# A 3-D average pooling kernel: the first load moved ahead of the sync engine's register instructions

## The chip, the cores and the metric

The kernel runs on one core of one Trainium2 chip. The time is the device time of one execution in microseconds (us), as the median of several executions. I compare only executions that alternated in one session on one chip.

## The reference

```python
def setup_inputs():
    batch, channels, d, h, w = (8, 32, 32, 32, 32)
    kernel_size = 2
    ...
# each output is the mean of a 2x2x2 window:
result[:, :, i, j, k] = np.mean(window, axis=(-3, -2, -1))
```

In: 33.55 MB of float32. Out: 4.19 MB.

## The kernel before

The 256 (batch, channel) rows fill 128 partitions twice. Each half is read in pieces of up to 128x8192 elements (4 MB), all issued by SyncE (SP) on one queue into five buffers. VectorE does three passes on each piece: add pairs along depth (line 58), pairs along width (line 62), pairs along height with the factor 0.125 (line 65). Three stores follow.

```python
    for t, k0, parts in plan:
        tin = pool_in.tile([P, 32 * KF], F32, tag="tin", name="tin")
        ...
            nc.sync.dma_start(                      # line 77: the ten loads
                out=v, in_=xv[t * P:(t + 1) * P, (k0 + o) * KF:(k0 + o + kb) * KF])
        ...
            pool_unit(v, t, k, kb)                  # VectorE, three passes
    for t, k0, kb in [(0, 0, 16), (1, 0, 14), (1, 14, 2)]:
        nc.sync.dma_start(...)                      # line 86: the three stores
```

While the source edits it, the program opens with a common block: six register instructions on each engine (a zero, the core's base address, four bounds), then a barrier of all engines. The kernel already lifts its first load, which waits for nothing, out of the program into that opening block, just ahead of SP's part of the barrier (SP's drain):

```python
    opening, program = blocks[0].instructions, blocks[tc.starting_block_idx].instructions
    load = next(i for i in program if isinstance(i, mybir.InstDMACopy))
    assert load.engine == nc.sync.engine
    barrier = next(
        n for n, i in enumerate(opening)
        if i.engine == load.engine and isinstance(i, mybir.InstDrain))
    program.remove(load)
    opening.insert(barrier, load)
```

Of the kernel before, what the change touches and what calls it, by code (L numbers as in the profile page):

```python
# [1 line left out]

# [4 lines left out]

F32 = mybir.dt.float32
KF = 256


@with_exitstack
def pool_rows(
    ctx: ExitStack,
    tc: tile.TileContext,
    x: bass.AP,
    kernel_size: int,
    out: bass.AP,
):
    nc = tc.nc  # L20
    assert kernel_size == 2, "only kernel_size == 2 supported"

    B, C, D, H, W = x.shape
    P = nc.NUM_PARTITIONS
    assert (B * C, D, H, W) == (2 * P, 32, 32, 32)
    add = mybir.AluOpType.add



    xv = x.rearrange("b c d h w -> (b c) (d h w)")  # L30
    ov = out.rearrange("b c d h w -> (b c) (d h w)")




    pool_in = ctx.enter_context(tc.tile_pool(name="pin", bufs=5))
    pool_out = ctx.enter_context(tc.tile_pool(name="pout", bufs=1))
    obuf = [pool_out.tile([P, 16 * KF], F32, name=f"obuf{t}") for t in range(2)]
    dummy = pool_out.tile([P, 1], F32, name="dummy")


    plan = [
        (0, 0, (32,)),
        (0, 32, (32,)),
        (0, 64, (32,)),
        (0, 96, (32,)),
        (1, 0, (32,)),
        (1, 32, (32,)),
        (1, 64, (16, 16)),
        (1, 96, (16, 16)),  # L50
    ]

    def pool_unit(buf, t, k0, kb):

        od = kb // 8
        a = buf.rearrange("p (o dd e) -> p o dd e", o=od, dd=2)
        b = buf[:, :od * 1024]
        nc.vector.tensor_add(  # L58
            out=b.rearrange("p (o e) -> p o e", o=od), in0=a[:, :, 0], in1=a[:, :, 1])
        bv = b.rearrange("p (e ww) -> p e ww", ww=2)  # L60
        c = buf[:, od * 1024:od * 1536]
        nc.vector.tensor_add(out=c, in0=bv[:, :, 0], in1=bv[:, :, 1])  # L62
        cv = c.rearrange("p (j hh k) -> p j hh k", hh=2, k=16)
        o0 = k0 * KF // 8
        nc.vector.tensor_tensor_reduce(  # L65
            out=obuf[t][:, o0:o0 + od * 256].rearrange("p (j k) -> p j k", k=16),
            in0=cv[:, :, 0], in1=cv[:, :, 1],
            scale=0.125, scalar=0.0, op0=add, op1=add, accum_out=dummy[:, :],
        )

    for t, k0, parts in plan:
        tin = pool_in.tile([P, 32 * KF], F32, tag="tin", name="tin")
        views = []
        o = 0
        for kb in parts:
            v = tin[:, o * KF:(o + kb) * KF]
            nc.sync.dma_start(
                out=v, in_=xv[t * P:(t + 1) * P, (k0 + o) * KF:(k0 + o + kb) * KF])
            views.append((v, k0 + o, kb))
            o += kb  # L80
        for v, k, kb in views:
            pool_unit(v, t, k, kb)


    for t, k0, kb in [(0, 0, 16), (1, 0, 14), (1, 14, 2)]:
        nc.sync.dma_start(
            out=ov[t * P:(t + 1) * P, k0 * KF:(k0 + kb) * KF],
            in_=obuf[t][:, k0 * KF:(k0 + kb) * KF],
        )


def kernel(tc: tile.TileContext, x: bass.AP, kernel_size: int, out: bass.AP):
    nc = tc.nc
    pool_rows(tc, x, kernel_size, out)
    tc.close()
    tc.compile()  # L96
    blocks = nc.main_func.blocks



    opening, program = blocks[0].instructions, blocks[tc.starting_block_idx].instructions
    load = next(i for i in program if isinstance(i, mybir.InstDMACopy))
    assert load.engine == nc.sync.engine
    barrier = next(
        n for n, i in enumerate(opening)
        if i.engine == load.engine and isinstance(i, mybir.InstDrain))
    program.remove(load)
    opening.insert(barrier, load)


# [1 line left out]
_INS = ['x', 'kernel_size']  # L112
_OUTS = [((8, 32, 16, 16, 16), 'float32')]

_NUMBERS = {'kernel_size': 2}


# [26 lines left out]
```

## Time and profile before

| | before |
|---|---|
| median of 3 executions | 93.52 us (93.45 to 93.53) |
| profiled execution | 93.1 us, span 91.3 us |
| transfers | 37.75 MB, 413 GB/s over the span |
| VectorE busy | 64.0 us, 70% of the span |
| first load | issued at 0.00, landed at 12.05 us |

The span runs from the first recorded instruction to the last; the device time is some 1.8 us longer (93.1 against 91.3). How to read it: the transfers are busy from end to end, VectorE waits for loads, and the chain that ended last begins with the load that the change moves. The prediction shows the lines.

### The profile page before, as it was taken

What the parts mean: (1) busy time and instruction counts of PE and PEld (TensorE: products, weight loads), DVE (VectorE), ACT (ScalarE), POOL (GpSimd) and SP (SyncE); (2) the same over time, 40 slices, a digit from 0 to 9 for tenths busy, and PEclk for the clock granted to TensorE, in tenths of its full rate; (3) what the DMA queues carried; (4) which work ended last, traced back from release to release, by engine and by line L of the source; (5) the groups of instructions that cost most, each with busy time, mean ns of one, the idle gap of its engine ahead of it and who ended that gap; (6) DMA issues with size and microseconds to landing.
All of it is one profiled execution on the core that took longest, in us unless ns stands there. A gap on an engine that the chain in (4) does not pass through costs nothing.

```text
span 91.3 us, 103 instructions
## 1 busy us (share of the span) xinstructions
DVE 64.0 (70%) x40; POOL 0.2 (0%) x4
## 2 busy tenths in 40 slices
DVE  0000079974999299939995699749999999999300
POOL 0000000000000000000000000000000000000000
DMA  8998799999997899999997999989999999999992
GB/s 230 459 445 373 344 445 459 459 459 459 459 445 344 373 445 459 459 459 459 459 431 330 388 459 459 459 345 459 445 395 423 459 431 395 409 409 436 427 395 84
DMA packets 1872, 37.75 MB, mean 413 GB/s; under 512 B 208, under 2 KB 208, under 8 KB 336
## 3 DMA queue, kind: packets, MB, share of 16 engines
q1 hardware_dynamic: 1872, 37.75, 97.2%
HBM read 33.55 MB, written 4.19 MB: 413 GB/s over the span
## 4 chain that ended last, share of the span: by engine, by line
DMA 58%; DVE 35%; issue 0%; DVEq 0%
DMA tin<-in_x_dram 58%; DVE tin L58 19%; DVE tin L62 10%; DVE obuf L65 6%; DVE dummy L65 0%; DVEq L96 0%
## 5 line engine op out<-in xcount | busy, mean ns | idle before, releaser
L58 DVE TENSOR_TENSOR tin<-tin 128x4096 f32<-128x4096 f32 (+1 forms) x10 | 35.7, 3569 | 20.5 <-DMA tin<-in_x_dram 20.5
L62 DVE TENSOR_TENSOR tin<-tin 128x2048 f32<-128x2048 f32 (+1 forms) x10 | 18.6, 1864 | 0.3
L65 DVE CUSTOM_DVE_ANT_1 obuf<-tin 128x1024 f32<-128x1024 f32 (+1 forms) x10 | 10.1, 1011 | 0.3
L65 DVE DVE_READ_ACCUMULATOR2_ANT dummy<- 128x1 f32 x10 | 0.8, 82 | 0.0
L125 POOL MEMSET const-bfloat16-1.0<- 128x1 bf16 x1 | 0.1, 101 | 0.0
L125 POOL MEMSET const-uint8-127<- 128x1 uint8 x1 | 0.1, 101 | 0.0
L125 POOL MEMSET const-float32-0.0<- 128x1 f32 x1 | 0.1, 98 | 0.2 <-issue 0.2
L125 POOL MEMSET const-float32-1.0<- 128x1 f32 x1 | 0.1, 98 | 0.0
## 6 DMA issues: line engine op xcount, KB each, us to landing
tin<-in_x_dram SPq DMA_DIRECT2D x6, 4096.0 KB, 34.9
tin<-in_x_dram SPq DMA_DIRECT2D x4, 2048.0 KB, 38.0
out_dram<-obuf SPq DMA_DIRECT2D x1, 2048.0 KB, 36.2
out_dram<-obuf SPq DMA_DIRECT2D x1, 1792.0 KB, 8.8
out_dram<-obuf SPq DMA_DIRECT2D x1, 256.0 KB, 5.1
```

Source lines behind the costliest of these rows:

```text
L58: nc.vector.tensor_add(out=b.rearrange("p (o e) -> p o e", o=od), in0=a[:, :, 0], in1=a[:, :, 1])
L62: nc.vector.tensor_add(out=c, in0=bv[:, :, 0], in1=bv[:, :, 1])
L65: nc.vector.tensor_tensor_reduce(out=obuf[t][:, o0:o0 + od * 256].rearrange("p (j k) -> p j k", k=16), in0=cv[:, :, 0], in1=cv[:, :, 1], s ...
L125: nc = _bacc.Bacc("TRN2", target_bir_lowering=False, num_devices=1)
```

## The change

The intent is to start the first transfer sooner by taking it past the six register instructions that stand ahead of it on SP.

```diff
     load = next(i for i in program if isinstance(i, mybir.InstDMACopy))
-    assert load.engine == nc.sync.engine
-    barrier = next(
-        n for n, i in enumerate(opening)
-        if i.engine == load.engine and isinstance(i, mybir.InstDrain))
+    assert load.engine == nc.sync.engine and load.regs_accessed() == ((), ())
+    assert not load.sync_info.on_wait
+    first = next(n for n, i in enumerate(opening) if i.engine == load.engine)
     program.remove(load)
-    opening.insert(barrier, load)
+    opening.insert(first, load)
```

## The prediction

> **What bounds the kernel now.** I read the page first (span, slices, chain), then the chain in order of time, then a table of stretches, and last what stands around the opening. The first view is the page of the kernel before:
>
> ```profile
> span 91.3 us, 103 instructions
> DVE 64.0 (70%) x40; POOL 0.2 (0%) x4
> ...
> DMA  8998799999997899999997999989999999999992
> ...
> HBM read 33.55 MB, written 4.19 MB: 413 GB/s over the span
> ...
> DMA 58%; DVE 35%; issue 0%; DVEq 0%
> ```
>
> To see here: the DMA engines are 7 to 9 tenths busy in 39 of 40 slices, VectorE only 70% of the span. The kernel is a stream of 37.75 MB through one DMA queue. The chain of waits in order of time says which work carries the end:
>
> ```profile
> 0.00 12.05 DMA tin<-in_x_dram
> ...
> 20.12 40.49 DMA tin<-in_x_dram
> 60.61 0.02 issue
> 60.63 4.44 DVE tin L58
> ```
>
> The columns are start, duration, what. The chain starts at 0.00 with the very load that the change touches, and 12.05 us pass until it has landed and VectorE may begin. The piece at 20.12 is the sixth load, released by the first tile's last VectorE instruction; its landing at 60.61 starts the last uninterrupted VectorE stretch. The table of stretches (start:end, length, DVE busy, POOL busy, clock, DMA share, GB/s) completes it:
>
> ```profile
> 0.00:2.00 2.00, 0.00 (x0) 0.20 (x4) 1.00 0.93 262
> 2.00:12.00 10.00, 0.00 (x0) 0.00 (x0) 1.00 0.97 419
> 12.00:22.00 10.00, 8.18 (x5) 0.00 (x0) 1.00 0.97 419
> 22.00:60.60 38.60, 31.57 (x16) 0.00 (x0) 1.00 1.00 431
> 60.60:85.20 24.60, 24.29 (x20) 0.00 (x0) 1.00 1.01 426
> 85.20:91.30 6.10, 0.00 (x0) 0.00 (x0) 1.00 0.67 283
> ```
>
> From 2.0 to 85.2 us the transfers run at 419 to 431 GB/s with no hole. In 60.6 to 85.2 VectorE is busy too (24.29 of 24.60 us), but that stretch begins with a landing. So the whole schedule hangs on the moment of the first issue: if the first load starts d earlier against the launch, I expect the end nearly d earlier. The slope is 1; the question is how large d is.
>
> **What the skill says.** (1) "Perfetto Trace Analysis", section "Per-instruction lifecycle: what the profiler-reported window actually captures", says that a hardware-generated DMA's window on the issuing queue covers only locking the descriptor generator, generating, and the sequencer's semaphore push, with the data movement outside. The trace agrees: the ten loads' issue windows are 327 to 501 ns (rows of line 77), while landing takes 12.1 us for the first. Moving an issue therefore moves the 12 us behind it, not just some 0.4 us. (2) The same page, section "Roofline", gives 16 DMA engines about 435 GB/s together. The stretches at 419 to 431 sit just below; single slices of the page show 459, so the measurement is the one to take, and it says that the stream is full. (3) "Runtime: NRT & Kernel Launch", section "Instruction fetch mechanics", puts a register loaded from HBM at about 200 ns. That bears on one of the six instructions, which loads the core's base address into two registers; the other five are register moves. No row of this trace is such a load, so the trace neither confirms nor denies it.
>
> **The change part by part.** It removes no work and adds none. In the kernel's own list of the opening, the first load stands behind SP's six register instructions and ahead of SP's drain; the change puts it ahead of the six.
>
> Step 1, is anything left to be jumped over? I compared the programs that the two kernels are built to, engine by engine. On SP both read: the load, a drain, a semaphore wait, a branch, then the other 12 transfers. The six register instructions are in neither: nothing in this program reads those registers, and they are gone when the program is written out. The compiled instruction streams of all five engines are the same byte for byte; only line numbers for debugging differ (the new source is one line shorter). The load was moved ahead of instructions that do not survive.
>
> Step 2, does the trace agree? The rows of line 125 (the opening barrier) and the head of the timeline:
>
> ```profile
> 0.00 2.66 SPq L77 DMA_DIRECT2D tin<-in_x_dram  x5
> 0.23 0.10 POOL L125 MEMSET const-float32-0.0<- 128x1 f32 x1 [0.23 <-issue]
> ```
>
> ```profile
> L125 DVEq DRAIN  x1: 10/10/10, 0.1 to 0.1; - x1
> L125 ACTq DRAIN  x1: 8/8/8, 0.1 to 0.1; - x1
> L125 SPq DRAIN  x1: 142/142/142, 0.4 to 0.4; - x1
> ```
>
> The load is the first record of the whole execution, ahead of the other engines' first drains at 0.1. And the page's 103 instructions can be added up: 40 on VectorE, 4 memsets, 12 other rows at line 125, 13 at line 77 (10 loads, 3 waits), 5 at line 86 (3 stores, 2 waits), 29 at line 96 (the closing barriers). 40 + 4 + 12 + 13 + 5 + 29 = 103, with no register instruction among them. A count alone would not prove it, since a profile may leave such instructions out; with the streams being equal it is enough.
>
> Step 3, the sum: instructions removed in front of the load 0, so d = 0 us. Off the path: nothing changes either. 93.52 us - 0 = 93.5 us.
>
> **The rivals.** Rival A: the six do run before and the load really gains their time. Size, an estimate: SP's closing waits and drains (line 96) follow one another about 65 ns apart in the trace (the first wait at 90.3 us, the sixth row at 90.6), so five moves are 0.3 us; the base load adds two registers at the 200 ns of the "Runtime" page, 0.4 us. d would be about 0.7 us and the time 92.8 us, still within 2% (which begins below 91.65 us). Against it: the built streams. Rival B: issued as the very first instruction, the load meets a queue or a descriptor generator that is not ready, and costs up to some tenths: 93.6 to 94.0. Against it: it is SP's first instruction already in the trace of before. Rival C: d is real but hidden, because the barrier of the opening or VectorE's tail sets the end. The barrier is over by 0.7 us, and the five first issues by 2.66, far ahead of the landing at 12.05, so it would stay hidden; it makes 93.5 as well and differs from my theory only if there is a d. Rival D: the same program simply times differently on another chip or at another hour. This is the only one that I think can show: the three runs spread 93.45 to 93.53, and the run under the profiler took 93.1, 0.4 us lower.
>
> **Range and chances.** The centre is the median of before. The width is only repetition: 0.08 us within one set, 0.4 us to the profiled run. I take 93.2 to 93.8. For faster or slower by over 2% something would have to move by 1.87 us, more than twice Rival A's whole estimate and more than four times the seen spread. I leave 1% on either side for a disturbed set of runs.
>
> **What would show it.** Right: in the profile after, 103 instructions again, the load at 0.00 and the first drains of the other engines at 0.1, VectorE's first instruction near 12.1 us, a span within 0.3 us of 91.3, and the opening rows of the same durations. Rival A would show as a first drain of the other engines clearly later against the load (0.7 instead of 0.1 us) and a time near 92.8. Rival B would show a first landing later than 12.3 us after the issue. I would be wrong if times differ by over 0.3 us in the same session in alternating runs while the streams are equal: then the premise that equal streams take equal time fails, for instance through where the program or its arrays lie in memory.

## The result, and the profile after

| | before | after |
|---|---|---|
| median, first session, 6 executions each | 93.43 us (93.2 to 93.53) | 93.49 us (93.35 to 93.71) |
| span of the profiled execution | 91.3 us | 91.9 us |

The ratio is 1.0012 with a 95% interval of 0.9993 to 1.0032, so the time is the same. A ratio here is the mean time of one kernel's fast runs over that of the other's of the same rounds, so it is not quite the ratio of the medians quoted.

From the page after, with the same fields as the lines of before:

```profile
span 91.9 us, 103 instructions
DVE 64.1 (70%) x40; POOL 0.2 (0%) x4
...
DMA  8999889999999988999999987999999999999992
...
HBM read 33.55 MB, written 4.19 MB: 411 GB/s over the span
```

Again 103 instructions. The head of the timeline (start, duration, queue, line, operation):

```profile
0.00 2.61 SPq L77 DMA_DIRECT2D tin<-in_x_dram  x5
0.23 0.10 POOL L124 MEMSET const-float32-0.0<- 128x1 f32 x1 [0.23 <-issue]
```

And the opening's rows, which are now line 124 because the source is one line shorter (count, durations in ns as min/median/max, first and last start):

```profile
L124 DVEq DRAIN  x1: 10/10/10, 0.1 to 0.1; - x1
L124 ACTq DRAIN  x1: 8/8/8, 0.1 to 0.1; - x1
L124 SPq DRAIN  x1: 133/133/133, 0.4 to 0.4; - x1
```

The load stands at 0.00 in both executions, and the other engines' drains follow at 0.1 in both. In the single records behind these rows, the starts of the next nine after the load differ by 1 or 2 ns between the two kernels; the tenth, SP's drain, starts at 432 ns in both and lasts 133 instead of 142 ns. Nothing was jumped over.

The two profiled executions differ by 0.6 us nevertheless, and one should know where. Two tables of stretches (start:end, length, DVE busy, POOL busy, clock, DMA share, GB/s), before:

```profile
12.00:60.00 48.00, 39.75 (x20) 0.00 (x0) 1.00 0.99 429
60.00:75.00 15.00, 14.26 (x10) 0.00 (x0) 1.00 1.00 427
75.00:80.00 5.00, 4.93 (x5) 0.00 (x0) 1.00 1.01 410
80.00:85.00 5.00, 4.90 (x6) 0.00 (x0) 1.00 0.99 426
```

After:

```profile
12.00:60.00 48.00, 39.74 (x20) 0.00 (x0) 1.00 0.99 428
60.00:75.00 15.00, 14.31 (x10) 0.00 (x0) 1.00 1.02 429
75.00:80.00 5.00, 4.93 (x5) 0.00 (x0) 1.00 1.01 370
80.00:85.00 5.00, 4.71 (x6) 0.00 (x0) 1.00 0.98 419
```

Up to 75 us the two are alike; the first landing is even 0.05 us earlier after (12.00 against 12.05). The difference arises between 75 and 80 us, while the last load is under way: 370 against 410 GB/s. The last load landed at 81.11 us after and at 80.48 before. It is not a property of the change: over the nine profiled executions the first nine landings, counted from the first issue, agree within 0.4 us, while the tenth lies anywhere between 80.5 and 81.1.

The DMA share of that stretch is 1.01 in both tables: the engines were not short of work, their packets took longer. A packet of the last loads takes 0.61 us (median). In all nine profiles, 15 to 31 of them took 0.70 to 1.28 us instead, and nearly all of these started between 76.7 and 79.4 us: 15 in before, which has the earliest tenth landing, and 26 in after, which has the latest. The last landing of the whole program then follows the tenth load by 9.81 to 9.83 us in all nine. So the lateness goes straight through to the end by the transfers, while VectorE ends only 0.22 us later (85.42 against 85.20).

This small lateness alters the look of the chain of waits. After:

```profile
0.73 0.07 issue
0.79 0.33 SPq L77
1.13 0.05 issue
1.18 30.24 DMA tin<-in_x_dram
...
39.86 41.25 DMA tin<-in_x_dram
81.11 0.02 issue
81.13 2.30 DVE tin L58
```

In before's chain, VectorE's last stretch began at 60.63. Here VectorE idled 0.2 us for the last load, so the chain is followed back through that load instead, and its share for transfers goes from 58% to 78%. A reader who compared only these shares would see a new bottleneck. Both chains belong to one schedule: the last load lands 0.44 us before VectorE asks for it in the one, and 0.2 us after in the other. Neither chain shows the end itself, which is the stores' landing at 90.31 and 90.93 us.

### The profile page after: what moved, and what is told of

The parts are those of the page before. It is cut to its first block, busy times and chain, and to the rows that moved or that the text cites. A ratio compares the mean times of both kernels' runs of the same rounds, so it can differ in the third digit from the quotient of the medians.

```text
span 91.9 us, 103 instructions
## 1 busy us (share of the span) xinstructions
DVE 64.1 (70%) x40; POOL 0.2 (0%) x4
## 4 chain that ended last, share of the span: by engine, by line
DMA 78%; DVE 13%; SPq 1%; issue 0%; DVEq 0%
DMA tin<-in_x_dram 78%; DVE tin L58 7%; DVE tin L62 4%; DVE obuf L65 2%; SPq L77 1%; DVE dummy L65 0%; DVEq L96 0%
```

## The experiments

The theory: the compiled streams are equal, so the change does nothing (the instruction files of all five engines are the same byte for byte); the first issue sets the end one for one, and what comes behind it has slack. Rivals: a small real effect hidden in the spread; register instructions that cost nothing anyway; early delays that are made up later; a barrier or a queue depth that matters.

**1. The changed kernel again, five alternating rounds.** No edit.

> The changed kernel once more, unaltered, five alternating rounds. My theory (the compiled streams are the same byte for byte, so the change does nothing): ratio to the kernel before within 0.3% of 1 on either side, profile with 103 instructions, other engines' first drains 0.1 us after the load. Rival (the change has a small real effect, of either sign, hidden by the first session's spread of 93.2 to 93.7): the same sign as in the first session, ratio about 1.0012, with an interval that leaves out 1.

Measured: 93.43 us (6 executions) against 93.46 us (11 executions of before). Ratio 0.9993, interval 0.9977 to 1.0009. The sign turned round against the first session and both intervals hold 1. There is no small effect that these runs can see.

**2. The six register instructions kept, ahead of the load.** This asks whether the idea would have been right if there had been something to jump over. The edit to the kernel before gives the registers a reader at the program's end. That reader is itself an empty instruction and is gone from the built program, but the six writers stay:

```diff
+    sp = nc.sync
+    base = sp.tpb_base_reg
+    regs = [sp.zero_reg, base.lo, base.hi] + [r for p in sp.bc_regs for r in (p.lo, p.hi)]
+    sp.keepalive_nop([sp.lower_val_access(r) for r in regs])
```

> The kernel before, with an empty instruction at the program's end that reads the seven registers, so that SP's six register instructions stay in the program and stand ahead of the load, as the intent of the change takes them to. If the six are costly and all that was missing is that they had been removed: slower than the kernel before by about 0.7 us (my estimate: five moves of 65 ns and one base load of 0.4 us), so about 94.2 us. Rival (register instructions cost SP next to nothing, or the measured time begins only with the first transfer): within 0.2 us of the kernel before. If the profile records register instructions, its count rises from 103 to 109.

Measured: 93.71 us against 93.46 us, ratio 1.0026, interval 1.0006 to 1.0046 (0.06 to 0.43 us). The page and the opening's rows show the six:

```profile
span 91.9 us, 109 instructions
```

```profile
L130 SPq MOVE  x5: 29/29/36, 0.0 to 0.3; - x5
...
L130 SPq BASE_LOAD  x1: 12/12/12, 0.1 to 0.1; - x1
...
L130 SPq DRAIN  x1: 128/128/128, 0.8 to 0.8; - x1
```

```profile
0.37 2.60 SPq L77 DMA_DIRECT2D tin<-in_x_dram  x5
12.42 4.43 DVE L58 TENSOR_TENSOR tin<-tin 128x4096 f32<-128x4096 f32 x1 [12.42 <-DMA tin<-in_x_dram]
```

So the profile does record register instructions: 103 + 6 = 109. The count of 103 in before therefore shows by itself that none ran there. The load's issue moved from 0.00 to 0.37 us, and VectorE's first instruction from 12.08 to 12.42. Neither of my two numbers fits well. The cost is real (0.25 us between the medians, 0.37 us at the issue, which the interval holds), but it is half or less of my 0.7 us.

**3. The six kept, the load first.** The same edit on the changed kernel.

> The changed kernel with the same six kept: the load first, then the six, then the drain. This is the change with something to jump over. My theory: the time of the kernel before within 0.2 us, since the six now run while the first load's bytes are on the way, and only delay the opening barrier and loads 2 to 5 (needed at 12 us and later). Rival (the opening barrier matters as well): slower than the kernel before by the six's cost, as much as the sibling with the six ahead.

Measured: 93.36 us against 93.46 us, ratio 0.9987, interval 0.9971 to 1.0003. The opening's rows and the timeline:

```profile
L129 SPq MOVE  x5: 29/29/40, 0.4 to 0.8; - x5
...
L129 SPq BASE_LOAD  x1: 49/49/49, 0.5 to 0.5; - x1
```

```profile
0.00 2.99 SPq L77 DMA_DIRECT2D tin<-in_x_dram  x5
...
12.01 4.42 DVE L58 TENSOR_TENSOR tin<-tin 128x4096 f32<-128x4096 f32 x1 [12.01 <-DMA tin<-in_x_dram]
```

The six now run from 0.4 to 0.8 us, behind the load, and cost nothing that can be measured. Runs 2 and 3 differ only in the place of the load, as the two kernels were meant to: 93.71 - 93.36 = 0.35 us, close to the 0.37 us of the shifted issue, and their intervals against before do not overlap. So in this kernel with its register instructions kept alive, the change would have worked and been worth about 0.4%; each of the two medians rests on six executions that spread over 0.4 to 0.7 us.

**4. The load not lifted at all.** The statements that lift the load are removed from the kernel before; nothing else changes.

```diff
-    opening, program = blocks[0].instructions, blocks[tc.starting_block_idx].instructions
-    load = next(i for i in program if isinstance(i, mybir.InstDMACopy))
...
-    program.remove(load)
-    opening.insert(barrier, load)
```

> The load is not hoisted at all: it stays the first instruction of the program, behind the opening barrier. It measures the slope: what a known delay of the first issue costs at the end. The issue comes some 0.6 to 0.8 us later than in the kernel before. Theory (one full stream of transfers, slope 1): the time rises by about that much, to 94.1 to 94.3 us. Rival (the delay is absorbed by VectorE's tail or a faster start of the queue): under 0.2 us.

Measured: 94.13 us against 93.46 us, ratio 1.0072, interval 1.0056 to 1.0087 (0.52 to 0.81 us). The timeline:

```profile
0.73 2.35 SPq L77 DMA_DIRECT2D tin<-in_x_dram  x5
12.87 4.42 DVE L58 TENSOR_TENSOR tin<-tin 128x4096 f32<-128x4096 f32 x1 [12.87 <-DMA tin<-in_x_dram]
```

Issue 0.73 us later, end 0.67 us later. The slope of about 1 holds for a delay of known size.

**5. A long register chain ahead of the load, and 6. the same chain behind it.** Both edit the changed kernel; the two differ in one line. A first attempt with additions only was folded to a single instruction by the build; alternating additions and multiplications are packed six to an instruction.

```diff
+    count = sp.alloc_register("count")
+    sp.reg_mov(count, 0)
+    for n in range(ADDS):                       # ADDS = 96
+        (sp.reg_mul if n % 2 else sp.reg_add)(count, count, 3)
+    sp.keepalive_nop([sp.lower_val_access(count)])
...
+    at = opening.index(load)                    # behind: opening.index(load) + 1
+    opening[at:at] = chain
```

> The changed kernel with a dependent chain of 96 additions and multiplications of one register (kept alive by a reader at the program's end; the build packs six into one instruction, so one move and 16 instructions) ahead of the load. It doubles or more the delay of the six register instructions (0.37 us in the run with the six ahead). Let X be the time from the first record to the load's issue, read from this run's profile; at 50 to 200 ns for each packed instruction X is 0.9 to 3.3 us. Theory (slope 1): the time is 93.4 us plus X within 0.3 us. Rival (part of an early delay is made up later): clearly less than X.

> The same chain directly behind the load, ahead of SP's drain. Theory (only the first issue is on the path): 93.4 us within 0.3 us, although the opening barrier and loads 2 to 5 come X later, as long as load 2 is issued before load 1's last packets at some 11 us. Rival (the barrier or the depth of the queue matters): slower by up to X.

Measured, against 93.25 us for the kernel before in the same rounds: ahead 95.38 us, ratio 1.0214, interval 1.0189 to 1.024 (1.76 to 2.24 us; clear of 1); behind 93.46 us, ratio 1.0013, interval 0.9993 to 1.0033. The timelines, ahead first:

```profile
1.96 2.66 SPq L78 DMA_DIRECT2D tin<-in_x_dram  x5
14.14 4.43 DVE L59 TENSOR_TENSOR tin<-tin 128x4096 f32<-128x4096 f32 x1 [14.14 <-DMA tin<-in_x_dram]
```

```profile
0.00 4.45 SPq L78 DMA_DIRECT2D tin<-in_x_dram  x5
...
12.11 4.42 DVE L59 TENSOR_TENSOR tin<-tin 128x4096 f32<-128x4096 f32 x1 [12.11 <-DMA tin<-in_x_dram]
```

X is 1.96 us. The interval against before holds it (the medians differ by 2.13 us), and ahead minus behind is 95.38 - 93.46 = 1.92 us: the slope once more. The 50 to 200 ns for a packed instruction in the expectation was a guess; they start 115 ns apart. Behind the load, the same chain makes the issues of loads 1 to 5 last until 4.45 instead of 2.66 us and delays the barrier with them, and no change of the time is seen. What lies behind the first issue is off the path.

**7. All five free loads ahead of the barrier.** An attempt to gain on both kernels.

```diff
+    loads = [i for i in program if isinstance(i, mybir.InstDMACopy)][:5]
...
+    opening[first:first] = loads
```

> The changed kernel with all five loads that wait for nothing ahead of the opening barrier. Theory: 93.4 us within 0.2 us, since the loads behind the first one have some 10 us to spare and the first one is where it was. Rival (a deeper queue in the first microseconds fills the slow start of the transfers, whose first packets take 1.9 instead of 1.2 us): 92.8 to 93.2 us.

Measured: 93.37 us against 93.25 us, ratio 1.0008, interval 0.9987 to 1.003. The five issues end at 2.37 instead of 2.66 us, and it brings nothing. The rival falls: the first 16 packets still take 1.43 to 2.19 us (1.30 to 2.10 in before), so the queue's slow start is not for want of loads behind the first. No run pointed to a version that beats both kernels, so there is none here.

Four starts of the first load in one table. The end is the landing of the last store, counted from the first issue, in the profiled execution. The medians come from three sessions (before had 93.46 and 93.25 us in the other two), so compare them only roughly:

| kernel | first issue, us | last landing after it, us | median, us |
|---|---|---|---|
| before (first profile) | 0.00 | 90.3 | 93.52 |
| six kept, ahead | 0.37 | 90.5 | 93.71 |
| not lifted | 0.73 | 90.7 | 94.13 |
| chain ahead | 1.96 | 90.8 | 95.38 |

The other five profiles have the issue at 0.00 and end 90.6 to 90.9 us after it. The spread of 90.3 to 90.9 is the spread of repetition described above; the rest of the schedule simply moves with the first issue.

## Why the prediction was right

- **Step 1 (nothing left to jump over) was right.** Giving the six a reader brought them back (run 2). The equal streams gave equal times within 0.12% in two sessions, with opposite signs.
- **Step 2 (the trace agrees) was right, and stronger than I claimed.** I held that a count of 103 would not prove it, since the profile might leave register instructions out. Run 2 shows that it records them.
- **Step 3 (d = 0, 93.5 us) was right:** 93.49 us, in the range.
- **The slope of 1 was right:** 0.73 us gave 0.67 us, and 1.96 us gave 1.92 us against the sibling kernel.
- **One of its signs did not come true:** a span within 0.3 us of 91.3. It was 91.9, with equal streams. I had taken the span of the one before profile as the mark, but that profile has the earliest end of all nine (90.3 us after the first issue; the others 90.5 to 90.9). So this sign could not tell the change from repetition.
- **The single slices of 459 GB/s were misread.** The page books a whole packet to the slice in which it starts, and 32 packets of 32 KB in a slice of 2.28 us make 459. Landings tell the rate better: loads 2 to 6 land 9.7 us apart, which is 432 GB/s, below the 435 that the prediction cites.
- **Rival A was mis-sized.** Two terms of it: five moves at 65 ns, and 0.4 us for the base load. In run 2 the records start at 0, 93, 140, 194, 253, 304 ns and the load at 374 ns; so the six cost 0.37 us, about 62 ns each. From the base load's start to the next start it is 47 ns in run 2 and 85 ns in run 3, where moves take 51 to 97 ns. The 200 ns that I took from the "Runtime" page is for a register loaded from memory, and two of those do not fit this instruction.
- **Rival B** (a queue that is not ready) shows no sign. The first load landed 11.99 to 12.12 us after its issue in the runs where it was SP's first instruction, and 12.02 (run 2), 12.12 (run 4) and 12.16 us (run 5) where others had run before it.
- **Rival C** (a real d, hidden by the barrier or VectorE's tail) fell, and the prediction argued it badly: that the barrier is over long before the landing means that it can't hide anything. Runs 3 and 6 delay the barrier and change nothing that can be seen; runs 2, 4 and 5 delay the first issue, and it shows.
- **Rival D was what remained.** The difference of 0.6 us between the two profiled executions came from the last load. Why some of its packets are slow is open. The first store is issued at 49.2 us already, but its packets do not coincide with the slow ones: loads 1 to 10 are 1280 data packets, and the 1281st starts at 79.58 us in before and 80.28 in after, later than all the slow ones.

## What to carry to other kernels

Before costing a reordering, compare the programs that come out of the build, not the lists that the source edits: instructions can be dropped afterwards, and then the diff reorders nothing. In this kernel, one stream of transfers from end to end, a delay of the first issue by up to 1.96 us came out at the end about one for one, and up to 1.8 us more work behind it in the opening cost nothing that could be seen. When two profiles of equal programs differ, look up in a table of stretches where, before trusting the shares of a chain of waits.

## What the Trainium skill lacked or had wrong

- "Runtime: NRT & Kernel Launch", section "Instruction fetch mechanics", gives about 200 ns for a register loaded from memory, but neither it nor any other page that I read has the cost of a register move or of the base load on SP. Measured: records of 29 to 40 ns for a move and 12 or 49 ns for the base load, 62 ns (run 2) and 69 ns (run 3) from start to start on average over the six; a packed instruction of six arithmetic operations mostly has a record of 74 ns and comes every 115 ns.
- No page that I read says that the register instructions of the opening vanish when nothing reads them: 103 recorded instructions without a reader, 109 with one.
- "DMA: Bandwidth & Descriptors", section "Specifications", gives about 0.6 us of first-byte latency for transfers that SP issues. Here the first packet began 1.00 to 1.03 us after the start of the issue's record, in all nine profiles. The two may be counted from different points.
- "Perfetto Trace Analysis", section "Per-instruction lifecycle: what the profiler-reported window actually captures", is borne out, so nothing is wrong there: a load's record is 327 to 524 ns long over the nine profiles, and the first landing comes 12.0 to 12.2 us after its start in all of them.
